# A decoder trunk in split fp32: the gated block's high part one flush later, weight sums a tile earlier, and a new order for the operand of layer 1

## The chip, the core and the metric

The kernel is one program on one core of a Trainium2 chip. A core has TensorE (PE in the profile, its weight loads PEld), VectorE (DVE), ScalarE (ACT), GpSimd (POOL) and SyncE (SP, which issues nearly all DMAs here). Each engine works through its own instructions in the order in which the program issues them; engines wait for each other through semaphores. The metric is the device time of one execution in microseconds (us), as a median over runs.

## What is computed

One inference step of a two-layer decoder for two request groups that share the weights: 1024 prompt positions and 8 x 8 sample positions, so T = 1088 columns of D = 1024 channels.

```python
for layer in range(DEPTH):                       # DEPTH = 2
    hn = rms_norm(h, norm_mix_g[layer])
    if layer % 2 == 0:                           # convolution module + stick-breaking attention
        mix, ... = conformer_sb_mixer(hn, ...)
    else:                                        # gated short convolution + causal pooling
        mix, ... = shortconv_pool_mixer(hn, ...)
    h = h + mix
    h = h + swiglu(rms_norm(h, norm_ffn_g[layer]), w_ffn_in[layer], w_ffn_out[layer])
y = rms_norm(h, norm_final_g)

def swiglu(h, w_in, w_out):
    g, u = jnp.split(h @ w_in, 2, axis=-1)
    return (jax.nn.silu(g) * u) @ w_out          # FFN_DIM = 2816
```

All inputs and outputs are fp32. Besides `y` the step returns the new keys, values and convolution and pooling states.

## The kernel before

**Split operands.** A product of fp32 operands is made as three matmuls: each operand is a high part (ScalarE's copy into the matmul format) and a low part (the operand minus its high part, by GpSimd for weights and by VectorE for activations), and `mm3` adds high by high, high by low and low by high. Activations lie with channels on the 128 partitions and positions in the free dimension. The columns are worked on as two groups, `GA` (512 columns, one block of 512) and `GB` (576 columns, two blocks of 288), in the mixer of layer 1 as one group `GT` of 1088.

**Weights.** `loads` lists every weight tile of 512 KB in the order of use, `seq` every operand made from them. `w_load` has SP fetch a tile into one of four `stage` buffers as soon as the tile that had the buffer has been read. `w_split(upto)` makes the operands `hl` (three buffers): L177 on ScalarE and L179 on GpSimd for a plain tile. `w_next` hands out the next operand and calls `w_split` so far that the operand two places on is split; so an operand is split while TensorE works two tiles before it.

**The gated channel mixer** (`run_ffn`). There are 22 tiles of 128 hidden channels, f = 0 to 21, taken in pairs. In a plain tile one product makes the gate and one the up part; VectorE scales each out of PSUM (L270, `scaled`), ScalarE takes the sigmoid-weighted gate, and `gated` puts a closure into the list `post`: multiply gate and up part on GpSimd (L430), high part on ScalarE (L431), and, put into the list `late`, low part on VectorE (L432). `flush` runs what stood in both lists when it was called; what is put into `late` meanwhile runs at the next flush. After each pair of tiles come two output tiles with four blocks each of the pair before (`out_block`, then `added`, L274 on VectorE, which adds the block to the residual `hb`), with a flush after the second block.

**Fast units.** From f = 5 on (`PLAIN`) a tile in layer 0 for `GB` and in layer 1 for both groups is made by seven products of half size instead of eight (`strassen`), 51 units in all. Its weights come as four forms r = 0 to 3 from one gate tile `sg` and one up tile `su`: sums and differences that VectorE makes (L186, L187, L188 for form 0, L191 for form 2) and then splits like other weights (L194 on ScalarE, L195 on GpSimd). The seven products (L452) fill four accumulators in this order: X (two products, form 0), Y (two, form 1), Z (two, form 2), W (one, form 3). ScalarE copies one half of Y (L468), and VectorE adds the products up in seven adds (L456): four need X and Y, two need Z, the last needs W. In program order the first four stand after Z's weights have been called for, the other three after W's. A flush stands between X and Y. There are three accumulators in PSUM, so a product waits until one is read out.

**Layer 1's operand** (`to_mixer`). With the last eight output blocks of layer 0 for `GB`, each finished channel tile n of `hb` is parked in memory, squared, and made into `x1[n]`: `prep` issues ScalarE's high part (L351) and queues VectorE's low part (L354) in `lowq`, once for the columns of `GB` and once for those of `GA`; `low(n)` works the queue down to n entries.

Of the kernel before, what the change touches and what calls it, by code (L numbers as in the profile page):

```python
# [8 lines left out]
F = mybir.dt.float32  # L9
# [9 lines left out]
NS = 64  # L19
# [10 lines left out]
def f32(ap):  # L30
    return ap.bitcast(F)
# [27 lines left out]
def trunk_kernel(ctx, tc, x_prompt, x_sample, cache_k, cache_v, state_conformer, state_shortconv, state_pool,  # L59
# [36 lines left out]
    def pc(c):  # L96
        return par[:, c:c + 1]
# [70 lines left out]
    def w_split(upto):  # L168
        while nxt[1] < min(upto, len(seq)):
            i = nxt[1]  # L170
            w_load(need(i + 1))
            a, b, r = seq[i]
            hl = wpool.tile([128, 2, 1024], FR, name="hl", bufs=3)
            lo, hi = slice(0, 512), slice(512, 1024)
            if b is None:
                st = stage.pop(a)
                act.activation(hl[:, 0], st, AF.Copy)  # L177
                for c in (lo, hi):
                    pool.tensor_tensor(hl[:, 1, c], st[:, c], f32(hl[:, 0, c]), op=OP.subtract)  # L179
                hls[i] = hl.rearrange("p s (k n) -> p s k n", k=loads[a][1])  # L180
            else:
                sg, su = stage[a], stage[b]
                if r == 0:
                    sums["a"], sums["b"] = (sums["p"].tile([128, n], F, name=f"sum{n}") for n in (1024, 512))
                    sa, sb = sums["a"], sums["b"]
                    dve.tensor_tensor(sb[:, lo], su[:, lo], su[:, hi], op=OP.add)  # L186
                    dve.tensor_tensor(sa[:, hi], sg[:, lo], su[:, lo], op=OP.subtract)  # L187
                    dve.tensor_tensor(sa[:, lo], sb[:, lo], sg[:, lo], op=OP.subtract)  # L188
                sa, sb = sums["a"], sums["b"]
                if r == 2:  # L190
                    dve.tensor_tensor(sa[:, hi], sg[:, hi], sa[:, lo], op=OP.subtract)  # L191
                src = ((sa[:, lo], sa[:, hi]), (sb[:, lo], sg[:, lo]), (su[:, hi], sg[:, hi]), (sa[:, hi],))[r]
                for c, x in zip((lo, hi), src):
                    act.activation(hl[:, 0, c], x, AF.Copy)  # L194
                    pool.tensor_tensor(hl[:, 1, c], x, f32(hl[:, 0, c]), op=OP.subtract)  # L195
                if r == 3:
                    stage.pop(a), stage.pop(b)
                hls[i] = hl.rearrange("p s (f k n) -> p s f k n", f=2, k=4)
            nxt[1] += 1

    wj = [0]

# [75 lines left out]
    late = []  # L278

    def flush():  # L280
        todo, low_parts = post[:], late[:]
        post.clear()
        late.clear()
        for f in todo + low_parts:
            f()

    K0 = list(range(KC))
# [58 lines left out]
        while len(lowq) > n:  # L346
            lowq.pop(0)()

    def prep(g, x, n, gain, squares=False, c0=0):
        o, i = x[n][:, :, c0:c0 + g.n], hb[:, n, g.cs]  # L350
        act.activation(o[:, 0], i, AF.Copy, scale=gain)  # L351
        if squares:
            add_squares(g, i, n == 0)
        lowq.append(lambda: dve.scalar_tensor_tensor(o[:, 1], i, gain, f32(o[:, 0]), op0=OP.mult, op1=OP.subtract))  # L354
# [47 lines left out]
    def run_ffn(g, accs, ps, hidp, x, last, sig=False, slot=lambda: None, forms=None):  # L402
        G = NF // 2
        n = g.n
        hid = {}
        gate = {}

        def ev_g(a):
            t = tmp()
            scaled(g, t[:, :n], a)  # L410
            if sig:
                s = tmp()
                act.activation(s[:, :n], t[:, :n], AF.Sigmoid)
                pool.tensor_tensor(t[:, :n], t[:, :n], s[:, :n], op=OP.mult)
            else:
                act.activation(t[:, :n], t[:, :n], AF.Silu)  # L416
            gate["t"] = t

        def ev_u(f, a):
            t = tmp()  # L420
            scaled(g, t[:, :n], a)
            gated(f, t, gate.pop("t"))

        def gated(f, t, u):
            if f // 2 not in hid:
                hid[f // 2] = hidp.tile([128, 2, 2, n], FR, name="hid")
            dst = hid[f // 2][:, f % 2]

            def fin():
                pool.tensor_tensor(t[:, :n], t[:, :n], u[:, :n], op=OP.mult)  # L430
                act.activation(dst[:, 0], t[:, :n], AF.Copy)  # L431
                late.append(lambda: dve.tensor_tensor(dst[:, 1], t[:, :n], f32(dst[:, 0]), op=OP.subtract))  # L432
            post.append(fin)

        def one(f, which):
            h = w_next()
            a = accs()
            block(g, a, h, x, slot=slot)
            flush()
            ev_g(a) if which == 0 else ev_u(f, a)  # L440
            slot()

        def strassen(f):
            w2 = n // 2

            def prod(acc, h, i, b):
                for k in range(4):
                    xk = forms[b](k)  # L450
                    for s, (wi, xi) in enumerate(((0, 0), (0, 1), (1, 0))):
                        pe.matmul(acc[:, :w2], h[:, wi, i, k], xk[:, xi], start=k == 0 and s == 0,  # L452
                                  stop=k == 3 and s == 2)

            def add(out, acc, x):
                dve.tensor_tensor(out, acc[:, :w2], x, op=OP.add)  # L456

            a, b = slice(0, w2), slice(w2, n)
            X, h = accs(), w_next()
            prod(X[:, 0], h, 0, "t2")  # L460
            prod(X[:, 1], h, 1, "t3")
            flush()
            slot()
            Y, h = accs(), w_next()
            prod(Y[:, 0], h, 0, "t1")
            prod(Y[:, 1], h, 1, "b11")
            G_, U, P = tmp(), tmp(), tmp()
            act.activation(G_[:, a], Y[:, 1, :w2], AF.Copy)  # L468
            Z, h = accs(), w_next()
            prod(Z[:, 0], h, 0, "t4")  # L470
            add(U[:, a], X[:, 0], G_[:, a])
            add(U[:, b], X[:, 1], U[:, a])
            add(P[:, b], Y[:, 0], U[:, b])
            add(G_[:, b], Y[:, 0], U[:, a])
            prod(Z[:, 1], h, 1, "b21")
            W, h = accs(), w_next()
            prod(W[:, 0], h, 0, "b22")
            add(P[:, a], Z[:, 0], U[:, b])
            add(G_[:, a], Z[:, 1], G_[:, a])
            add(G_[:, b], W[:, 0], G_[:, b])  # L480
            act.activation(G_[:, :n], G_[:, :n], AF.Silu)
            gated(f, P, G_)
            slot()

        for q in range(G + 1):
            if q < G:
                for f in (2 * q, 2 * q + 1):
                    if forms and f >= PLAIN:
                        if f == PLAIN:
                            forms["switch"]()  # L490
                        strassen(f)
                        continue
                    if f == 0:
                        run_in(g, accs, x, [ev_g, lambda a: ev_u(0, a)], norm_hooks(g, ps))
                        slot()
                        continue
                    one(f, 0)
                    one(f, 1)
            if q == G:
                flush()  # L500
                flush()
                last(hid.pop(q - 1))
            elif q:
                hh = hid.pop(q - 1)
                for o in range(2):
                    h = w_next()
                    for i in range(4):
                        a = accs()
                        out_block(g, a, h, i, hh)
                        added(g, hb[:, o * 4 + i, g.cs], a)  # L510
                        if o == 0 and i == 1:
                            flush()
                        slot()
# [745 lines left out]
    acc_pool(GA, 3)  # L1259
    hstack = ExitStack()  # L1260
    hidp = hstack.enter_context(tc.tile_pool(name="hid0", bufs=2, side="right"))
    knew = consts.tile([128, 4, NS], F, name="knew")
    act.activation(knew, kall[:, :, SEQ:T], AF.Copy)

    def flow_c():
# [49 lines left out]
    def to_mixer(hh):  # L1315
# [9 lines left out]
        for o in range(2):  # L1325
            h = w_next()
            for i in range(4):
                n = o * 4 + i
                a = accs()
                out_block(GB, a, h, i, hh)  # L1330
                added(GB, hb[:, n, GB.cs], a)
                sp.dma_start(park[:, n, GB.cs], hb[:, n, GB.cs])
                add_squares(GB, hb[:, n, GB.cs], n == 0)
                prep(GB, x1, n, pc(MIXG + 8 + n), c0=HALF)
                low(1)
                prep(GA, x1, n, pc(MIXG + 8 + n))
                behind.append(lowq.pop())
        low()
        for f in behind:
            f()  # L1340
# [386 lines left out]
```

## Time and profile before

| | us |
|---|---|
| median of 3 runs (lowest, highest) | 2681.61 (2680.7, 2682.34) |
| the profiled execution, its own time | 2677.37 |
| span of the profiled execution, first to last instruction | 2675.2 |
| TensorE busy in it | 2540.1 |
| VectorE, GpSimd, ScalarE busy | 1637.9, 1569.5, 1084.8 |
| mean granted TensorE clock | 0.988 |

A row of the timeline has the start, the length, the engine, the line of the kernel, what is written from what with its shape, and how many instructions are merged (x12); in brackets stand the idle time of the engine ahead of it and what ended that. A row of the list of waits has who waited for whom, the total in us, how often, and the longest wait. A row of groups has the count, the busy time, the mean in ns, and the idle time with its releasers. The row "GB/s" has the DMA rate in 40 equal slices of the window asked for.

### The profile page before, as it was taken

To read this page: it belongs to the slowest core of one execution; us is meant where nothing else is said; L and a number is where in the kernel's file an instruction comes from. 1 tells how busy PE (TensorE), PEld (TensorE's weight loads), DVE (VectorE), ACT (ScalarE), POOL (GpSimd) and SP (SyncE) were. 2 spreads that over 40 slices of the span, in tenths; PEclk is the share of its full clock that TensorE was granted. 3 is DMA by queue.
4 is the path that set the end of the run, shared out by engine and by line. 5 is a ranking of instruction groups with operands and counts; after the bars stand their busy time and mean duration, and the time that the engine had idled before them with its cause. 6 is when DMAs were issued, how large, how long until landed. Compare 5 with 4: busy or idle time off the path is not lost. (4 is left out here: it accounts for less than half of the span.)

```text
span 2675.2 us, 40716 instructions
## 1 busy us (share of the span) xinstructions
PE 2540.1 (95%) x15627; PEld 2257.4 (84%) x15627; DVE 1637.9 (61%) x2262; ACT 1084.8 (41%) x1814; POOL 1569.5 (59%) x1199
## 2 busy tenths in 40 slices
PE   8989998999999998999999899999999999999998
PEld 6788877887666656999999899998788888999997
DVE  3774776868756634377666633333666676666665
ACT  5436766744343324343333422122333334333333
POOL 6756244444333337478788722234788887677875
PEclk9999999999999999999999999999999999999999
DMA  7332241234445434322332411131232333233232
GB/s 218 114 97 71 62 112 36 71 112 117 142 142 152 119 110 128 89 72 80 95 95 87 128 44 40 42 113 34 87 93 87 90 95 95 67 104 107 85 90 75
DMA packets 346008, 254.06 MB, mean 95 GB/s; under 512 B 22657, under 2 KB 295169, under 8 KB 345800
## 3 DMA queue, kind: packets, MB, share of 16 engines
q1 hardware_dynamic: 345784, 251.46, 32.1%
q8 instruction: 124, 2.03, 0.3%
q14 instruction: 68, 0.56, 0.1%
q10 hardware_dynamic: 32, 0.01, 0.0%
HBM read 233.21 MB, written 18.69 MB: 94 GB/s over the span
## 5 line engine op out<-in xcount | busy, mean ns | idle before, releaser
L179 POOL TENSOR_TENSOR hl<-stage,hl 128x512 fp32r<-128x512 f32 x484 | 667.6, 1405 | 481.5 <-ACT hl L177 323.7
L214 PE MATMUL acc<-x,hl 128*128 128x288 f32 (+1 forms) x3792 | 710.1, 340 | 12.0 <-DVE hb L274 7.4
L214 PEld LDWEIGHTS acc<-x,hl 128*128 128x128 f32 x3792 | 585.0, 190 | 98.7 <-issue 35.3
L214 PE MATMUL acc<-hid,hl 128*128 128x288 f32 (+1 forms) x3072 | 551.0, 335 | 35.3 <-DVE hb L274 23.6
L214 PEld LDWEIGHTS acc<-hid,hl 128*128 128x128 f32 x3072 | 465.1, 190 | 105.8 <-DVE hb L274 35.1
L274 DVE TENSOR_TENSOR hb<-acc,hb 128x512 f32<-128x512 f32 (+2 forms) x376 | 263.6, 717 | 224.2 <-PE acc L214 222.1
L195 POOL TENSOR_TENSOR hl<-sum,hl 128x512 fp32r<-128x512 f32 x204 | 282.8, 1403 | 172.6 <-ACT hl L194 167.1
L452 PE MATMUL acc<-tt,hl 128*128 128x288 f32 (+1 forms) x2448 | 331.6, 291 | 0.6 <-ACT hl L194 0.3
L452 PEld LDWEIGHTS acc<-tt,hl 128*128 128x128 f32 x2448 | 321.0, 189 | 1.9 <-ACT hl L194 0.6
L177 ACT ACTIVATE hl<-stage 128x1024 fp32r<-128x1024 f32 x242 | 252.0, 1052 | 142.7 <-PE acc L214 100.9
L214 PE MATMUL acc<-x1t,hl 128*128 128x364 f32 (+1 forms) x1728 | 293.8, 331 | 7.4 <-DVE x1t L354 4.1
L214 PEld LDWEIGHTS acc<-x1t,hl 128*128 128x128 f32 x1728 | 288.9, 190 | 9.3 <-DVE x1t L354 4.4
L452 PE MATMUL acc<-x,hl 128*128 128x288 f32 (+1 forms) x1836 | 256.9, 292 | 18.0 <-ACT hl L177 12.9
L456 DVE TENSOR_TENSOR tmp<-acc,tmp 128x288 f32<-128x288 f32 (+1 forms) x357 | 146.5, 442 | 202.7 <-ACT tmp L468 157.9
L452 PEld LDWEIGHTS acc<-x,hl 128*128 128x128 f32 x1836 | 243.8, 190 | 20.8 <-ACT hl L177 19.2
L195 POOL TENSOR_TENSOR hl<-stage,hl 128x512 fp32r<-128x512 f32 x153 | 229.7, 1524 | 20.8 <-ACT hl L194 10.5
L270 DVE TENSOR_TENSOR tmp<-acc,rr 128x512 f32<-128x512 f32 (+3 forms) x128 | 89.7, 712 | 204.7 <-PE acc L214 189.2
L194 ACT ACTIVATE hl<-sum 128x512 fp32r<-128x512 f32 x204 | 122.1, 623 | 186.1 <-DVE sum L188 119.1
L431 ACT ACTIVATE hid<-tmp 128x512 fp32r<-128x512 f32 (+1 forms) x88 | 57.9, 657 | 326.6 <-POOL tmp L430 326.5
L231 POOL TENSOR_TENSOR ss<-ss,tmp 128x512 f32<-128x512 f32 (+2 forms) x62 | 105.2, 1696 | 87.8 <-ACT tmp L230 84.4
L430 POOL TENSOR_TENSOR tmp<-tmp 128x512 f32<-128x512 f32 (+1 forms) x88 | 125.7, 1429 | 26.4 <-ACT tmp L416 25.4
L214 PE MATMUL acc<-x1a,hl 128*128 128x512 f32 x480 | 121.3, 406 | 2.5 <-POOL hl L179 1.3
(252 smaller groups left out, 2936.4 us busy)
## 6 DMA issues: line engine op xcount, KB each, us to landing
stage<-in_w_ffn_in_dram SPq DMA_DIRECT2D x176, 512.0 KB
stage<-in_w_ffn_out_dram SPq DMA_DIRECT2D x88, 512.0 KB
stage<-in_w_in_even_dram SPq DMA_DIRECT2D x40, 512.0 KB
kst<-in_cache_k_dram SPq DMA_DIRECT2D x64, 256.0 KB
vst<-in_cache_v_dram SPq DMA_DIRECT2D x64, 256.0 KB
stage<-in_w_out_even_dram SPq DMA_DIRECT2D x16, 512.0 KB
stage<-in_w_in_odd_dram SPq DMA_DIRECT2D x16, 512.0 KB
park<-hb SPq DMA_DIRECT2D x16, 288.0 KB
```

Source lines behind the costliest of these rows:

```text
L177: act.activation(hl[:, 0], st, AF.Copy)
L179: pool.tensor_tensor(hl[:, 1, c], st[:, c], f32(hl[:, 0, c]), op=OP.subtract)
L194: act.activation(hl[:, 0, c], x, AF.Copy)
L195: pool.tensor_tensor(hl[:, 1, c], x, f32(hl[:, 0, c]), op=OP.subtract)
L214: pe.matmul(acc[:, b, :c1 - c0], w, x[:, xi, c0:c1], start=first and s == 0, stop=last and s == 2)
L231: pool.tensor_tensor(ss[:, g.cs], ss[:, g.cs], t[:, :g.n], op=OP.add)
L270: dve.tensor_tensor(d, a, r, op=OP.mult)
L274: dve.tensor_tensor(d, a, d, op=OP.add)
L430: pool.tensor_tensor(t[:, :n], t[:, :n], u[:, :n], op=OP.mult)
L431: act.activation(dst[:, 0], t[:, :n], AF.Copy)
L452: pe.matmul(acc[:, :w2], h[:, wi, i, k], xk[:, xi], start=k == 0 and s == 0, stop=k == 3 and s == 2)
L456: dve.tensor_tensor(out, acc[:, :w2], x, op=OP.add)
```

## The change

Three edits and a small one.

*Flush.* `fin` now issues only the multiply and puts both parts of the split into `late`, so that the high part (ScalarE) moves from right behind the multiply to the next flush, where it stands with the low part (VectorE). `flush` itself does what it did.

*Weight sums.* After an operand has been split, `w_split` looks at the next one. If that is a form 0, its tiles are called for and two of its three sums are issued there. The third sum stays at form 0. Form 2's sum gets a tile of its own (`sum_c`) where it used to overwrite half of `sum1024`.

*Layer 1's operand.* One high part over all 1088 columns takes the place of two; the low parts are queued for `GB` and `GA` of each channel tile, and from the third tile on `GA`'s is put off until all blocks are done. `prep` loses its argument `c0`.

*Memory.* `knew` moves from the constants into a pool that ends with layer 0's work on `GA`.

```diff
@@ w_split
             else:
                 sg, su = stage[a], stage[b]
+                sa, sb = sums["a"], sums["b"]
                 if r == 0:
-                    sums["a"], sums["b"] = (sums["p"].tile([128, n], F, name=f"sum{n}") for n in (1024, 512))
-                    sa, sb = sums["a"], sums["b"]
-                    dve.tensor_tensor(sb[:, lo], su[:, lo], su[:, hi], op=OP.add)
-                    dve.tensor_tensor(sa[:, hi], sg[:, lo], su[:, lo], op=OP.subtract)
                     dve.tensor_tensor(sa[:, lo], sb[:, lo], sg[:, lo], op=OP.subtract)
-                sa, sb = sums["a"], sums["b"]
                 if r == 2:
-                    dve.tensor_tensor(sa[:, hi], sg[:, hi], sa[:, lo], op=OP.subtract)
-                src = ((sa[:, lo], sa[:, hi]), (sb[:, lo], sg[:, lo]), (su[:, hi], sg[:, hi]), (sa[:, hi],))[r]
+                    sums["c"] = sums["p"].tile([128, 512], F, name="sum_c")
+                    dve.tensor_tensor(sums["c"], sg[:, hi], sa[:, lo], op=OP.subtract)
+                src = ((sa[:, lo], sa[:, hi]), (sb[:, lo], sg[:, lo]), (su[:, hi], sg[:, hi]), (sums.get("c"),))[r]
...
             nxt[1] += 1
+
+            a, b, r = seq[min(i + 1, len(seq) - 1)]
+            if b is not None and r == 0:
+                w_load(b + 1)
+                sg, su = stage[a], stage[b]
+                sums["b"] = sums["p"].tile([128, 512], F, name="sum512")
+                dve.tensor_tensor(sums["b"], su[:, lo], su[:, hi], op=OP.add)
+                sums["a"] = sums["p"].tile([128, 1024], F, name="sum1024")
+                dve.tensor_tensor(sums["a"][:, hi], sg[:, lo], su[:, lo], op=OP.subtract)
@@ gated
             def fin():
                 pool.tensor_tensor(t[:, :n], t[:, :n], u[:, :n], op=OP.mult)
-                act.activation(dst[:, 0], t[:, :n], AF.Copy)
-                late.append(lambda: dve.tensor_tensor(dst[:, 1], t[:, :n], f32(dst[:, 0]), op=OP.subtract))
+                late.append(lambda: split(dst, t[:, :n]))
             post.append(fin)
@@ to_mixer
                 add_squares(GB, hb[:, n, GB.cs], n == 0)
-                prep(GB, x1, n, pc(MIXG + 8 + n), c0=HALF)
+                gain = pc(MIXG + 8 + n)
+                act.activation(x1[n][:, 0], hb[:, n], AF.Copy, scale=gain)
+                for gr in (GB, GA):
+                    lowq.append(lambda gr=gr, n=n, gain=gain: dve.scalar_tensor_tensor(
+                        x1[n][:, 1, gr.cs], hb[:, n, gr.cs], gain, f32(x1[n][:, 0, gr.cs]), op0=OP.mult,
+                        op1=OP.subtract))
+                if n > 1:
+                    behind.append(lowq.pop())
                 low(1)
-                prep(GA, x1, n, pc(MIXG + 8 + n))
-                behind.append(lowq.pop())
         low()
         for f in behind:
             f()
```

More of the change, by code (lines that the diff above doesn't have):

```diff
@@ L280, in flush @@
     def flush():
-        todo, low_parts = post[:], late[:]
+        todo = post + late
         post.clear()
         late.clear()
-        for f in todo + low_parts:
+        for f in todo:
             f()
@@ L347, in low, with prep @@
             lowq.pop(0)()
-    def prep(g, x, n, gain, squares=False, c0=0):
-        o, i = x[n][:, :, c0:c0 + g.n], hb[:, n, g.cs]
+    def prep(g, x, n, gain, squares=False):
+        o, i = x[n][:, :, :g.n], hb[:, n, g.cs]
         act.activation(o[:, 0], i, AF.Copy, scale=gain)
@@ L1261, in trunk_kernel @@
     hidp = hstack.enter_context(tc.tile_pool(name="hid0", bufs=2, side="right"))
-    knew = consts.tile([128, 4, NS], F, name="knew")
+    knew = hstack.enter_context(tc.tile_pool(name="knewp", bufs=1, side="right")).tile([128, 4, NS], F, name="knew")
     act.activation(knew, kall[:, :, SEQ:T], AF.Copy)
```

## The prediction

> **What bounds the kernel now.** I read the page first, then the list of who waited for whom on TensorE, then the order of time in one period of each stage that the change touches.
>
> ```profile
> span 2675.2 us, 40716 instructions
> PE 2540.1 (95%) x15627; PEld 2257.4 (84%) x15627; DVE 1637.9 (61%) x2262; ACT 1084.8 (41%) x1814; POOL 1569.5 (59%) x1199
> ```
> ```profile
> PE acc L214 <- DVE hb L274: 34.0, 33, 5.2
> PE acc L452 <- ACT hl L177: 12.9, 9, 2.1
> PE acc L214 <- DVE x1t L354: 4.1, 1, 4.1
> ```
>
> PE is busy 95% of the span, so time can only come from its waits. The three above (total, count, longest) are what the change aims at: the output blocks that wait for `added` (L274), the last product of a fast unit in group A of layer 1, and the first low part of layer 1's operand.
>
> Below is one period of that group A stage. I call the four accumulators of a fast unit X, Y, Z, W, and the eight output blocks that follow every second unit o1 to o8. Three accumulators exist; by the order of release W takes X's, o1 Y's, o2 Z's, o3 W's, o4 that of o1.
>
> ```profile
> 2029.44 3.82 POOL L195 TENSOR_TENSOR hl<-sum,hl 128x512 fp32r<-128x512 f32 x3 [2.13 <-ACT hl L194]
> 2033.21 4.26 POOL L195 TENSOR_TENSOR hl<-stage,hl 128x512 fp32r<-128x512 f32 x3
> 2037.43 1.30 POOL L430 TENSOR_TENSOR tmp<-tmp 128x512 f32<-128x512 f32 x1
> 2039.99 1.27 POOL L195 TENSOR_TENSOR hl<-sum,hl 128x512 fp32r<-128x512 f32 x1 [1.26 <-ACT hl L194]
> 2041.26 5.93 POOL L179 TENSOR_TENSOR hl<-stage,hl 128x512 fp32r<-128x512 f32 x4
> ```
> ```profile
> 2036.85 1.60 PE L452 MATMUL acc<-tt,hl 128*128 128x256 f32 x12
> ...
> 2038.29 1.60 PE L452 MATMUL acc<-x,hl 128*128 128x256 f32 x12
> 2038.76 0.63 ACT L431 ACTIVATE hid<-tmp 128x512 fp32r<-128x512 f32 x1 [5.34 <-POOL tmp L430]
> 2039.30 0.61 ACT L194 ACTIVATE hl<-sum 128x512 fp32r<-128x512 f32 x1
> ...
> 2040.21 2.43 DVE L456 TENSOR_TENSOR tmp<-acc,tmp 128x256 f32<-128x256 f32 x6 [6.40 <-ACT tmp L468]
> 2041.24 1.66 PE L452 MATMUL acc<-x,hl 128*128 128x256 f32 x12 [1.36 <-ACT hl L177]
> ...
> 2042.74 4.42 PE L214 MATMUL acc<-hid,hl 128*128 128x512 f32 x18
> ...
> 2043.28 1.06 DVE L186 TENSOR_TENSOR sum<-stage 128x512 f32<-128x512 f32 x1
> ...
> 2044.27 1.77 DVE L187 TENSOR_TENSOR sum<-stage 128x512 f32<-128x512 f32 x1
> 2045.96 1.78 DVE L188 TENSOR_TENSOR sum<-sum,stage 128x512 f32<-128x512 f32 x1
> 2047.66 1.27 DVE L274 TENSOR_TENSOR hb<-acc,hb 128x512 f32<-128x512 f32 x2
> 2048.39 7.27 PE L214 MATMUL acc<-hid,hl 128*128 128x512 f32 x30 [1.24 <-DVE hb L274]
> ```
>
> The reader is to see two stalls. PE stands 1.36 us before W: ScalarE waits 5.34 us at L431 for GpSimd's multiply L430, its split L194 comes behind, and GpSimd's low part of that form ends only at 2041.26, when W starts (so I read the name L177 in the row as the wrong one). Then o1, o2, o3 run (18 matmuls, 1.33 us a block) and o4 stands 1.24 us, because VectorE makes three sums for the next unit (L186 to L188) before the first `added`.
>
> **The change part by part.** *Flush.* The high part moves from behind the multiply to the flush after it. In this period L431 leaves ScalarE's queue at that place; L194 can run as soon as X is done, and GpSimd's last low part follows L430 at once: 2037.43 + 1.30 + 1.27 = 2040.00 instead of 2041.26. Z's last product ends at 2038.29 + 1.60 = 2039.89. So W starts at 2040.0 and ends at 2041.4, and ScalarE's evacuation of Y (L468) no longer waits behind L431: Y is complete at 2036.9, and four adds of 0.41 us are done by about 2039.0.
>
> *Sums a tile ahead.* L186 and L187 are now issued when the second output tile is split, which is at the call for W's weights. On VectorE's in-order queue that is behind the first four adds and **ahead of the two adds that free Z**, while L188 stays ahead of `added`. What these sums need is the pair of weight tiles just being loaded:
>
> ```profile
> 2037.50 0.37 SPq L159 DMA_DIRECT2D stage<-in_w_ffn_in_dram  x1
> ```
> ```profile
> GB/s 0 0 0 0 0 76 139 160 254 293 334 348 338 258 209 182 209 287 311 301 240 135 53 43 25 0 0 0 0 0 0 0 0 33 0 41 76 190 266 317
> ```
>
> SP issues the second tile at 2037.50, when GpSimd has read the last of the old one (2033.21 + 4.26 = 2037.47). The second row is the DMA rate in quarter microseconds from 2036: bytes flow until 2042.25. The tile is thus there between 2042.25 and 2043.28, where L186 reads it today without a wait; I take 2042.65. Nothing in the change moves that issue: `w_load` for this pair was called earlier in both versions, and GpSimd's six splits from 2029.44 to 2037.47 stand back to back.
>
> So VectorE, idle from 2039.0, waits until 2042.65, and Z's two adds behind it. The sums have three prices: 1.06 and 1.77 above, both beside GpSimd, and 0.68 in this row of the last stage:
>
> ```profile
> 2396.88 0.68 DVE L186 TENSOR_TENSOR sum<-stage 128x512 f32<-128x512 f32 x1
> ```
>
> GpSimd's four L179 start 1.26 us earlier and still last until about 2045.9, so I take 1.5 + 1.77. Z is free at 2042.65 + 1.5 + 1.77 + 2 x 0.41 = 2046.75. PE has finished o1 at 2041.4 + 1.33 = 2042.75 and **stands about 4 us before o2**; o4 then begins at 2046.8 + 2 x 1.33 = 2049.5. Today it is 2048.39. Both old stalls go, one larger comes: **+1.1 us**. With sums at 1.06 + 1.2 and landing at 2042.25 it is -0.3, with 1.78 twice and landing at 2043.0, +1.7. Behind o4 nothing is late: L188 and `added` take 1.4 us after W's last add, and o4 wants them at 2049.4.
>
> [...]
>
> The same in layer 0, group B, and layer 1, group B:
>
> ```profile
> 1396.12 4.95 PE L214 MATMUL acc<-hid,hl 128*128 128x288 f32 x36
> 1401.48 0.80 PE L214 MATMUL acc<-hid,hl 128*128 128x288 f32 x4 [0.41 <-DVE hb L274]
> ```
> ```profile
> GB/s 0 0 0 20 113 174 242 322 303 301 332 240 201 207 215 223 317 320 285 158 125 119 12 0 0 0 0 0 0 0 0 0 0 0 8 94 158 190 299 317
> ```
> ```profile
> 2451.28 4.92 PE L214 MATMUL acc<-hid,hl 128*128 128x288 f32 x36
> ...
> 2451.86 1.83 DVE L186 TENSOR_TENSOR sum<-stage 128x512 f32<-128x512 f32 x1
> ...
> 2456.71 8.20 PE L214 MATMUL acc<-hid,hl 128*128 128x288 f32 x60 [0.51 <-DVE hb L274]
> ```
> ```profile
> GB/s 0 0 0 0 0 0 0 0 23 82 158 285 330 283 309 348 283 213 225 229 252 315 317 287 139 107 76 0 0 0 0 0 0 0 0 0 0 0 0 16
> ```
>
> There is no stall before W here, and a block takes 1.59 us. Bytes flow until 1394.75 (the row starts at 1389) and 2449.75 (it starts at 2443); with 0.4 us more the sums start at 1395.15 and 2450.15. Z is free 1.5 + 1.77 + 0.9 later, at 1399.3 and 2454.3; two blocks on, o4 begins at 1402.5 and 2457.5 instead of 1401.48 and 2456.71: **+1.0 and +0.8 us**.
>
> Each stage has eight such places: 8 x (1.1 + 1.0 + 0.8) = +23.2. Two of the eight in the last stage lie beside transposes of finished rows and have no stall today:
>
> ```profile
> 2378.76 3.33 PE L214 MATMUL acc<-hid,hl 128*128 128x288 f32 x24
> ```
> ```profile
> GB/s 0 0 139 352 221 328 131 145 223 205 188 236 227 258 277 264 311 346 336 324 324 225 129 33 18 2 0 0 0 0 0 0 0 0 0 0 66 0 0 0
> ```
>
> There bytes flow until 2378.5, Z is free at about 2382.6, and o2 starts today at 2378.76 + 1.59 = 2380.35: 2.2 us instead of 0.8, twice +1.4. The last unit of group A has its stall before W and no sums behind it: -1.3.
>
> Before the *other* unit of a pair the sums keep their order on VectorE, since nothing of that engine stands between the old place and the new. The separate tile for the fourth form takes away a wait; the new flush adds one, L432 behind L431 in the same flush:
>
> ```profile
> L187 DVE TENSOR_TENSOR sum<-stage 128x512 f32<-128x512 f32 x51 | 63.4, 1243 | 29.7 <-POOL hl L195 29.7
> L431 ACT ACTIVATE hid<-tmp 128x512 fp32r<-128x512 f32 (+1 forms) x88 | 57.9, 657 | 326.6 <-POOL tmp L430 326.5
> ```
>
> 29.7 us over 51 sums, mostly 1.2 us in every second, against up to 0.66 us for the copy: behind L432 stand the sums and `added`. I set both at zero together, from -0.5 to +0.6 a pair. In the plain stages ScalarE gets the 3.7 us a flush back that it waits at L431, with PE hardly waiting for it: -2, from -8 to +6.
>
> *Layer 1's operand.*
>
> ```profile
> 1532.37 0.74 PE L214 MATMUL acc<-x1t,hl 128*128 128x364 f32 x3 [2.88 <-DVE hb L274]
> 1537.17 3.09 PE L214 MATMUL acc<-x1t,hl 128*128 128x364 f32 x9 [4.07 <-DVE x1t L354]
> ```
> ```profile
> 1531.22 0.67 ACT L230 ACTIVATE tmp<-hb 128x576 f32<-128x576 f32 x1
> ```
> ```profile
> L219 ACT ACTIVATE x1t<-hb x8: 1098/1102/1115, 1741.4 to 1749.2; 128x1088 fp32r<-128x1088 f32 x8
> ```
>
> PE runs three matmuls and stands 4.07 us for the first low part of group A's columns. The change makes that part early, so this wait goes. But ScalarE's one copy of 1088 columns (1.10 us by the like L219) precedes it, and in the first two columns VectorE must wait for square and copy of the same column (0.7 + 1.1) before its next `added`. Two such waits, 3.6 us, move the end of the eighth `added` from 1532.3 to 1535.9; PE starts at 1536.0 and runs on, where today's start at 1537.17 has three matmuls (0.5 us) behind it: -0.7, from -4.3 (all gained) to +2. `knew` only changes its pool: nothing.
>
> **Sum:** 23.2 + 2.8 - 1.3 - 2 - 0.7 = +22.0. The profiled execution took 2677.37 us (2.2 beside its span), 4.2 under the median of 2681.61; added to the median: **2703.6 us**.
>
> **The rivals.** *The sums find their tile* (faster). If both tiles were there when VectorE comes to them, the old stalls would simply go: in group A 8 x 2.6 + 1.4, in the group B stages some 14 x 0.45, with the last two terms -31: 2651. It decides at a landing before 2042.75 - 0.82 - 3.27 = 2038.7, four microseconds ahead of the rows; smaller gains come from sums at 0.68 each (o4 at 2047.5 in group A). For it: GpSimd's splits would have to move, and L187's lost wait frees up to 1.2 us of them. Against it: the rate rows. *Balance:* partly hidden sums (1.06 + 1.2) and an early landing, about 0 a place, which leaves the small terms: 2678. *VectorE late in every unit:* L432 waits 0.6 us in each of 24 pairs and L188, the next form and X come as much later: +14, 2718; against it, the wait lost at L187.
>
> **How the numbers follow.** About 0.2%, 5.4 us, is what a measurement can tell from no change. Forecast 0.56 (2690 to 2715), VectorE late 0.14, balance 0.16, faster 0.14. Slower is 0.70. The range, 2680 to 2722, leaves out the faster case and the ends: landing and sums at their bounds are worth -1.4 to +0.6 a place, -34 to +14 over 24, of which the lower half is given to the rivals.
>
> **What would show it.** Right: L186's successor starts with a wait for a DMA, ends ahead of the two Z adds (L456's successor), and PE stands 1 to 4 us before o2 with that add as releaser, 24 times; no stall before W in group A; no 4 us wait for x1t. Wrong: PE waits for `acc` shrink below 34 us, or VectorE reaches the sums after their tile.

## The result and the profile after

| | before | after |
|---|---|---|
| median of 4 runs (lowest, highest), us | 2681.15 (2680.61, 2682.34) | 2699.32 (2696.44, 2705.41) |
| ratio to before, 95% interval | | 1.007 [1.0051, 1.0089] |
| profiled execution, its own time, us | 2677.37 | 2697.51 |
| span, us | 2675.2 | 2695.6 |
| mean granted TensorE clock | 0.988 | 0.982 |

The change makes the kernel slower by 0.7%: 18.2 us by the medians, 20.4 by the spans. The forecast was +22.0 us (2703.6, range 2680 to 2722). The kernel after moves the lines: products are L457 (before L452), their seven adds L461 (L456), output blocks L220 (L214), `added` L280 (L274), `scaled` L276 (L270); the two sums made ahead are L203 and L205 (L186, L187), the third is L185 (L188).

The page after (the span, then the busy time of each engine):

```profile
span 2695.6 us, 40688 instructions
PE 2550.9 (95%) x15627; PEld 2269.7 (84%) x15627; DVE 1624.9 (60%) x2262; ACT 1089.1 (40%) x1806; POOL 1573.5 (58%) x1199
```

and TensorE's list of waits (who waited for whom, total, times, longest):

```profile
PE acc L220 <- DVE tmp L461: 42.3, 24, 3.6
PE acc L220 <- DVE hb L280: 19.3, 10, 5.2
```

All three waits that the change aimed at shrink or go: 34.0 to 19.3 us for `added`; the row of 12.9 us before W is gone (0.61 us is left, in group A's first fast unit), and so are the 4.1 us for layer 1's operand. In their place stands one that did not exist: 24 output blocks wait 42.3 us for VectorE's adds, at the 24 places where sums are made behind output tiles. PE is also *busy* 10.8 us longer with the same 15627 matmuls. A longer busy time at the same count needs a cause of its own; it comes below.

One period of group A in layer 1, first TensorE and then VectorE (start, length, what, and in brackets the idle time ahead and its releaser):

```profile
2040.71 3.04 PE L457 MATMUL acc<-x,hl 128*128 128x256 f32 x24
2043.59 1.57 PE L220 MATMUL acc<-hid,hl 128*128 128x512 f32 x6
2047.43 8.90 PE L220 MATMUL acc<-hid,hl 128*128 128x512 f32 x37 [2.28 <-DVE tmp L461]
```
```profile
2039.89 1.77 DVE L461 TENSOR_TENSOR tmp<-acc,tmp 128x256 f32<-128x256 f32 x4 [4.08 <-ACT tmp L473]
2044.34 0.70 DVE L203 TENSOR_TENSOR sum<-stage 128x512 f32<-128x512 f32 x1 [2.68 <-DMA stage<-in_w_ffn_in_dram]
2044.97 1.75 DVE L205 TENSOR_TENSOR sum<-stage 128x512 f32<-128x512 f32 x1
2046.64 1.07 DVE L461 TENSOR_TENSOR tmp<-acc,tmp 128x256 f32<-128x256 f32 x3
```

Z and W run as one group of 24 matmuls without a stall between them. VectorE has done four adds by 2041.66, stands 2.68 us for the weight tile, makes the two sums, and only then Z's adds. PE has finished o1 and stands 2.28 us before o2, released by such an add. This is the order that the prediction wrote down; its numbers differ, as shown below.

The same in layer 1's group B:

```profile
2470.51 1.75 PE L220 MATMUL acc<-hid,hl 128*128 128x288 f32 x12
2472.95 9.25 PE L220 MATMUL acc<-hid,hl 128*128 128x288 f32 x68 [0.69 <-DVE tmp L461]
```
```profile
2469.42 1.05 DVE L203 TENSOR_TENSOR sum<-stage 128x512 f32<-128x512 f32 x1 [1.14 <-DMA stage<-in_w_ffn_in_dram]
2470.39 1.77 DVE L205 TENSOR_TENSOR sum<-stage 128x512 f32<-128x512 f32 x1
```

and at a place beside transposes of finished rows:

```profile
2389.68 1.75 PE L220 MATMUL acc<-hid,hl 128*128 128x288 f32 x12
2393.76 2.98 PE L220 MATMUL acc<-hid,hl 128*128 128x288 f32 x12 [2.33 <-DVE tmp L461]
2396.53 1.06 PE L1617 MATMUL m<-ident,hb 128*128 128x128 f32 x4
2397.24 5.14 PE L220 MATMUL acc<-hid,hl 128*128 128x288 f32 x36
2402.22 0.60 PE L1617 MATMUL m<-ident,hb 128*128 128x128 f32 x4
```

Compare rows of one shape: twelve matmuls take 1.75 us before the stall and 2.98 us after it, and four transposes take 1.06 and, 6 us later, 0.60 us. The table of windows of this kernel (window, its length, busy time and count of PE, PEld, DVE, ACT, POOL, then the granted clock, DMA share and GB/s) shows why:

```profile
2388.00:2394.10 6.10, 3.77 (x28) 3.54 (x28) 4.44 (x6) 1.06 (x1) 4.05 (x3) 1.00 0.09 24
2394.10:2397.50 3.40, 3.40 (x17) 3.39 (x16) 1.96 (x4) 2.40 (x4) 2.01 (x2) 0.50 0.03 5
2397.50:2402.00 4.50, 4.50 (x36) 4.50 (x36) 3.26 (x5) 1.09 (x2) 2.79 (x3) 1.00 0.30 92
```

For 3.4 us behind the stall the granted clock is 0.50. PE is busy in all of it, but its matmuls of 288 columns start every 0.24 us there and every 0.13 us ahead of the stall and from 2397.6 us on, so such a stretch costs 1.5 us by that pitch, and up to 1.7 us by the clock alone. Adding up these stretches over the whole span, before has 62.9 us at half clock and after 96.7 us. But for the one that the end of the span cuts off, they come in lengths of 3.4 and 6.8 us. In the part of the trace with layer 1's fast units, after has nine such lengths that before has not: six in group A (one of them double) and three in group B, 30.6 us, worth up to 15.3 us. There they stand behind all four stalls of 3.25 to 3.6 us and behind four of the seven of 2.26 to 2.38 us, and behind none of the short ones (0.67 to 0.8 us). Layer 0 has one more of 2.34 us and seven of 0.67 to 1.96 us at these places, and none of them has half clock behind it.

Layer 1's operand, after:

```profile
1526.82 5.42 PE L220 MATMUL acc<-hid,hl 128*128 128x288 f32 x36 [1.35 <-DVE hb L280]
1537.27 8.93 PE L220 MATMUL acc<-x1t,hl 128*128 128x364 f32 x43 [5.03 <-DVE hb L280]
```

One stall of 5.03 us, with a new one of 1.35 us ahead of it, takes the place of 2.88 and 4.07 us: the 4 us wait went, and its time came back.

### The profile page after: what moved, and what is told of

It reads as the page before. It is cut to its first block, busy times and chain, and to the rows that moved or that the text cites. A ratio compares the mean times of both kernels' runs of the same rounds, so it can differ in the third digit from the quotient of the medians.

```text
span 2695.6 us, 40688 instructions
## 1 busy us (share of the span) xinstructions
PE 2550.9 (95%) x15627; PEld 2269.7 (84%) x15627; DVE 1624.9 (60%) x2262; ACT 1089.1 (40%) x1806; POOL 1573.5 (58%) x1199
## 5 line engine op out<-in xcount | busy, mean ns | idle before, releaser
L179 POOL TENSOR_TENSOR hl<-stage,hl 128x512 fp32r<-128x512 f32 x484 | 672.1, 1413 | 479.7 <-ACT hl L177 336.3
L220 PE MATMUL acc<-x,hl 128*128 128x288 f32 (+1 forms) x3792 | 708.3, 340 | 11.8 <-DVE hb L280 7.9
L220 PEld LDWEIGHTS acc<-x,hl 128*128 128x128 f32 x3792 | 584.0, 190 | 97.7 <-issue 38.4
L220 PE MATMUL acc<-hid,hl 128*128 128x288 f32 (+1 forms) x3072 | 567.4, 341 | 64.9 <-DVE tmp L461 42.3
L220 PEld LDWEIGHTS acc<-hid,hl 128*128 128x128 f32 x3072 | 479.4, 195 | 136.7 <-DVE tmp L461 49.3
L280 DVE TENSOR_TENSOR hb<-acc,hb 128x512 f32<-128x512 f32 (+2 forms) x376 | 268.4, 720 | 268.9 <-PE acc L220 267.4
L457 PE MATMUL acc<-tt,hl 128*128 128x288 f32 (+1 forms) x2448 | 331.6, 291 | 0.3 <-POOL hl L192 0.3
L457 PEld LDWEIGHTS acc<-tt,hl 128*128 128x128 f32 x2448 | 321.0, 189 | 1.3 <-POOL hl L192 0.5
L220 PE MATMUL acc<-x1t,hl 128*128 128x364 f32 (+1 forms) x1728 | 293.6, 331 | 5.5 <-DVE hb L280 5.0
L220 PEld LDWEIGHTS acc<-x1t,hl 128*128 128x128 f32 x1728 | 289.0, 190 | 7.0 <-ACT x1t L1340 5.2
L192 POOL TENSOR_TENSOR hl<-sum,hl 128x512 fp32r<-128x512 f32 x153 | 205.2, 1362 | 113.7 <-ACT hl L191 113.7
L457 PE MATMUL acc<-x,hl 128*128 128x288 f32 (+1 forms) x1836 | 253.0, 291 | 4.0 <-DVE tmp L461 3.3
L461 DVE TENSOR_TENSOR tmp<-acc,tmp 128x288 f32<-128x288 f32 (+1 forms) x357 | 146.8, 440 | 165.2 <-ACT tmp L473 122.1
L457 PEld LDWEIGHTS acc<-x,hl 128*128 128x128 f32 x1836 | 242.0, 189 | 4.6 <-ACT hl L177 3.8
L276 DVE TENSOR_TENSOR tmp<-acc,rr 128x512 f32<-128x512 f32 (+3 forms) x128 | 89.7, 712 | 185.3 <-PE acc L220 175.7
L191 ACT ACTIVATE hl<-sum 128x512 fp32r<-128x512 f32 x153 | 91.0, 626 | 124.2 <-PE acc L220 62.4
L191 ACT ACTIVATE hl<-stage 128x512 fp32r<-128x512 f32 x153 | 89.8, 618 | 118.3 <-PE acc L220 113.8
L226 DVE TENSOR_TENSOR hid<-tmp,hid 128x512 fp32r<-128x512 f32 (+1 forms) x88 | 97.4, 1107 | 61.6 <-ACT hid L225 60.3
```

Of the source, the lines that this page charges most:

```text
L220: pe.matmul(acc[:, b, :c1 - c0], w, x[:, xi, c0:c1], start=first and s == 0, stop=last and s == 2)
L226: dve.tensor_tensor(dst[:, 1], src, f32(dst[:, 0]), op=OP.subtract)
L276: dve.tensor_tensor(d, a, r, op=OP.mult)
L280: dve.tensor_tensor(d, a, d, op=OP.add)
```

## The experiments

Ten kernels ran, in three comparisons, each with the kernel before on the same chip.

| label | what it is | median, us (lowest, highest) | ratio to before, 95% interval |
|---|---|---|---|
| sums_only | before + the weight sums | 2697.43 (2691.07, 2699.19) | 1.0057 [1.0043, 1.0071] |
| flush_only | before + the flush | 2651.78 (2650.41, 2652.84) | 0.9889 [0.9874, 0.9904] |
| operand_only | before + the operand | 2678.78 (2674.97, 2681.72) | 0.9991 [0.9982, 1.0] |
| no_tile_wait | after, sums without their tile | 2644.43 (2641.11, 2648.39) | 0.9863 [0.9848, 0.9878] |
| flush_operand | after without the sums | 2653.23 (2650.54, 2655.88) | 0.9896 [0.9882, 0.991] |
| inner_only | after, sums ahead only inside a pair | 2653.01 (2648.45, 2657.31) | 0.9898 [0.9883, 0.9914] |
| between | flush, operand, sums among the blocks | 2658.83 (2650.11, 2660.72) | 0.9915 [0.9899, 0.993] |
| keep_clock | after + unread matmuls in group A | 2693.02 (2685.86, 2698.76) | 1.0046 [1.0031, 1.006] |
| keep_all | the same, and three places of group B | 2689.58 (2684.34, 2695.59) | 1.0037 [1.0024, 1.0049] |
| after_again | after, beside keep_all | 2705.36 (2696.11, 2706.54) | 1.0091 [1.0076, 1.0107] |

The kernel before had 2680.9 us in the comparison of the first four, 2680.71 in that of the next four, 2681.3 in that of the last two.

### One part at a time

**sums_only** is before with the edit of `w_split` and the move of `knew`.

> The kernel before with the sums a tile ahead (and form 2's own tile), nothing else. Theory: the whole loss comes from here. VectorE reaches L186's successor before the next weight tile has landed, two adds that free accumulator Z stand behind it, TensorE stands before the second output block, and where it stands over 2 us a half-clock window of 3.4 us follows: +10 to +25 us over the kernel before. Group A of layer 1 is the worst, since its stall before W stays as well. Rival (the flush makes the loss, by ScalarE's and VectorE's later split): within 4 us of the kernel before.

It ran at +16.5 us. Its list of waits (L220, L280 and L462 are output blocks, `added` and the seven adds; L458 is the products):

```profile
PE acc L220 <- DVE tmp L462: 29.3, 24, 3.3
PE acc L220 <- DVE hb L280: 18.1, 11, 5.2
PE acc L458 <- ACT hl L177: 9.3, 9, 2.1
```

So this one edit brings the 24 waits, and alone it makes nearly the whole loss. The stall before W, which this edit leaves, remains at 9.3 us. "Over 2 us" in the expectation says more than the trace of after: of its twelve stalls of 2.26 to 3.60 us at these places, eight have a stretch at half clock behind them.

**flush_only** is before with this:

```diff
-                act.activation(dst[:, 0], t[:, :n], AF.Copy)
-                late.append(lambda: dve.tensor_tensor(dst[:, 1], t[:, :n], f32(dst[:, 0]), op=OP.subtract))
+                late.append(lambda: split(dst, t[:, :n]))
```

> The kernel before with the high part of the gated block at the next flush, nothing else. Theory: the eight or nine stalls of 1.36 us before W in group A of layer 1 go, but the sums there start with the landing of their tile, so that most of it comes back before the fourth output block: -2 to -8 us against before, and TensorE's waits for L456 and L274 tell where. Rival (the flush makes the loss): +8 us or more, with TensorE waiting for units whose form 0 is late.

It ran at −29.1 us, far below what I expected. The same group A period, TensorE and then GpSimd (products L451 here):

```profile
2028.30 3.04 PE L451 MATMUL acc<-x,hl 128*128 128x256 f32 x24
2031.18 4.41 PE L214 MATMUL acc<-hid,hl 128*128 128x512 f32 x18
2036.98 7.26 PE L214 MATMUL acc<-hid,hl 128*128 128x512 f32 x30 [1.39 <-DVE hb L274]
```
```profile
2027.17 1.30 POOL L430 TENSOR_TENSOR tmp<-tmp 128x512 f32<-128x512 f32 x1
2028.42 1.30 POOL L195 TENSOR_TENSOR hl<-sum,hl 128x512 fp32r<-128x512 f32 x1
2029.67 5.51 POOL L179 TENSOR_TENSOR hl<-stage,hl 128x512 fp32r<-128x512 f32 x4
```

GpSimd goes from L430 to L195 without the 1.26 us that stand between them in the rows of before, Z and W are one group, and the stall before o4 is 1.39 us where it was 1.24. The stall before W, 1.36 us in most periods, is simply gained, in every period but the first (1.81 of 2.06 us are left there): from the first to the last fast unit of group A this kernel moves 11.3 us ahead of before, by the starts of the units' first products. In group B before has stalls before W only in the first two pairs of layer 0 (2.09, 0.67 and 0.48 us; here 1.72 and none) and in the first unit of layer 1 (1.62 us, here 1.61). Yet it gains in all of group B, 6.8 us in layer 0 (up to 1.7 of it a stretch at half clock that before alone has, at 1212.8 us) and 4.6 in layer 1. These three gains make 22.7 of the 24.3 us between the two profiled spans. VectorE in layer 1's group B:

```profile
2431.48 1.04 DVE L186 TENSOR_TENSOR sum<-stage 128x512 f32<-128x512 f32 x1
2432.44 1.77 DVE L187 TENSOR_TENSOR sum<-stage 128x512 f32<-128x512 f32 x1
2434.14 0.68 DVE L188 TENSOR_TENSOR sum<-sum,stage 128x512 f32<-128x512 f32 x1
```

L186 takes 1.04 us where it took 1.83 us at its counterpart of before (2451.86): GpSimd's low part ends 1.4 us earlier against the matmuls, and the sum meets GpSimd's next instructions at another point (L179 runs from 2430.69 to 2433.67 here, from 2449.35 to 2454.84 there); that this sets its time was not shown apart. The 0.8 us that this saves is more than the 0.51 us that o4 waited there. Half clock is 69.6 us here, 62.9 before, so the gain as a whole is no effect of the clock.

**operand_only** is before with the third edit.

> The kernel before with the one high part and late low parts of layer 1's operand, nothing else. Theory: the wait of 4.07 us for the first low part goes, and about as much comes back before it, because the last block's add is later: -2 to +1 us against before. Rival (a saving of the whole wait): -4 us.

11 runs differ from the kernel before by 2.1 us of 2681, which can't be told from no change, and at the place itself the tenth matmul of the operand moves by 0.05 us.

The parts alone sum to 16.5 − 29.1 − 2.1 = −14.7 us; together they give +18.2. The flush gains 29 us alone and nothing once the sums are made ahead (2699.3 for the whole change against 2697.4 for sums_only).

### Is it the landing of the tile?

**no_tile_wait** is after with

```diff
-                dve.tensor_tensor(sums["b"], su[:, lo], su[:, hi], op=OP.add)
+                dve.tensor_tensor(sums["b"], rr[:, lo], rr[:, hi], op=OP.add)
-                dve.tensor_tensor(sums["a"][:, hi], sg[:, lo], su[:, lo], op=OP.subtract)
+                dve.tensor_tensor(sums["a"][:, hi], rr[:, lo], rr[:, hi], op=OP.subtract)
```

where `rr` is a tile that is there all the time.

> The changed kernel, but the two sums that are made a tile ahead read columns of rr, which have been there for long, in place of the next unit's weight tiles (the same shapes on the same engine; the output is no longer the reference's). Theory: the sums no longer wait for a landing, TensorE's 42 us of waiting for L461 nearly goes, and most of the half-clock windows of layer 1 with it: 2650 to 2662 us. If only the time of the sums on VectorE's queue counts and not the landing: 2680 to 2695. Rival (the flush makes the loss): 2690 or more.

It runs 55 us below after, even below its range. Its longest list entries are

```profile
PE acc L220 <- DVE hb L280: 18.2, 8, 5.2
PE acc L220 <- DVE tmp L276: 13.8, 3, 5.6
PE acc L220 <- POOL hl L179: 7.3, 12, 1.3
```

and the row for L461 is not among them. The instructions and their order are those of after; only the tile that the two sums read differs, and with it the wait for its arrival. So it is the landing that costs, not the sums' own 2.5 us of VectorE.

**flush_operand** has `w_split` as it was; **inner_only** makes the sums ahead only where the operand before is itself a form, so at the 24 places behind output tiles, and at the first fast unit of each group, which follows a plain tile, they stand as before:

```diff
-            if b is not None and r == 0:
+            if b is not None and r == 0 and seq[i][1] is not None:
```

> The changed kernel with the sums put back to where they were (flush and operand stay). The parts alone gave -29 us (flush) and -2 us (operand) against before, and +17 us (sums), while all three together gave +18. Theory: the sums undo the flush's gain wherever a weight tile is late, so that without them flush and operand simply add: 2646 to 2653 us. Rival (flush and operand disturb each other): 2660 or more.

> The changed kernel, but the two sums are made a tile ahead only for the second unit of a pair, whose form 0 follows directly on a form 3; the first unit's, behind two output tiles, are made where they were. Theory: all of the harm lies at the 24 places behind output tiles, where the tile has not landed; the inner places have theirs: within 4 us of the run with the sums put back, 2644 to 2655. Rival (the sums ahead of time harm in every unit, by standing in front of adds): 2665 or more.

The two have the same time, 2653.2 (just above its range) and 2653.0. So sums ahead inside a pair cost and gain nothing, and all the harm, 46 us on top of the other two edits, lies at the 24 places: at the three first units TensorE stands no longer before Y and W in after (1.72, 0.90 and 1.63 us) than in flush_only (1.72, 1.81 and 1.61 us).

**between** tries to have the sums early without the queue: one sum after each of the first three blocks' `added`, and form 0 split behind the third block.

> Flush and operand as in the change; the three sums for the first unit of a pair are not made ahead but one after each of the first three output blocks' adds, and form 0 is split after the third. Theory: the tile has landed, and no add of a finished block waits behind three sums in a row, so that the 1.2 to 1.6 us stalls before the fourth block in group A of layer 1 shrink below 0.5: 8 to 11 us below flush and operand alone, 2636 to 2645. Rival (VectorE is simply too busy among the output blocks, and form 0 comes too late): no better than flush and operand alone.

That fell short. In its profile the stall before o4 is gone (one period has 0.30 us before o5), but each of the eight pairs in group A has 0.77 or 0.78 us inside one of its units (L467 is the products, L471 their adds):

```profile
2016.65 1.60 PE L467 MATMUL acc<-x,hl 128*128 128x256 f32 x12
2019.02 1.67 PE L467 MATMUL acc<-x,hl 128*128 128x256 f32 x12 [0.77 <-DVE tmp L471]
```

Its runs reach from 2650 to 2661 us, and its median is no better than that of flush_operand.

### Is half clock a cost, or a label beside the stall?

**keep_clock** gives PE something to do in the stalls of group A; **keep_all** does so at the first three places of layer 1's group B as well (the edit is keep_all's; `warm` lists the pairs):

```diff
+                        if o == 0 and i == 0 and q in warm:
+                            m = ps()
+                            for _ in range(16):
+                                pe.matmul(m[:, :256], h[:, 0, 0, 0:128], hh[:, 0, 0, 0:256], start=True, stop=True)
                         if o == 0 and i == 1:
                             flush()
```

> The changed kernel, with 16 matmuls of 256 columns that nothing reads put between the first and second output block at the eight places of group A in layer 1 (1.7 to 1.9 us of TensorE work at full clock, into a stall of 2.3 us). Theory of the clock: the stall itself costs little there, the half-clock window of 3.4 us that follows most of the stalls does; with TensorE kept busy those five or six windows between 1930 and 2240 us go, and the stage ends 4 to 10 us earlier in spite of more work. Rival (the clock windows cost nothing, the wait does): the stage ends when it did or up to 3 us later.

> The changed kernel with 16 matmuls of 256 columns that nothing reads between o1 and o2, at the eight places of layer 1's group A and at the first three of its group B. Theory (a stall of over 2 us brings a stretch of 3.4 us at half clock behind it, worth up to 1.7 us): in the stages from 1910 to 2475 us the nine stretches' worth (30.6 us) of half clock go, which is up to 15.3 us; the unread matmuls lie in the stalls, and what they cost beyond is 0 to 5 us. So 8 to 14 us below the changed kernel in the same comparison, about 2685 to 2692. Rival (the half clock is only a label beside a wait that would last as long anyway): the same time as the changed kernel or up to 10 us above it, since eleven times 1.7 us of matmuls are added.

> The changed kernel as it is, beside the one before it in this list and on the same chip, so that the two can be compared. Every theory: 2694 to 2706 us, ratio to the kernel before 1.005 to 1.009, with about ten more half clock stretches than the kernel before.

The windows from 1913 to 2473 us, first of after, then of keep_all:

```profile
1913.00:2473.00 560.00, 517.94 (x3484) 485.08 (x3482) 359.32 (x492) 209.37 (x338) 415.10 (x293) 0.97 0.30 88
```
```profile
1913.00:2473.00 560.00, 536.15 (x3759) 507.42 (x3759) 368.28 (x504) 214.39 (x347) 422.54 (x299) 1.00 0.30 89
```

The granted clock is 1.00 instead of 0.97, and over the whole span half clock falls from 96.7 us (in after and in after_again) to 64.0 us. keep_all runs 15.8 us below after_again on the same chip (12 by the two profiled executions), with intervals that lie apart, although it does 176 matmuls more; expected were 8 to 14. Of those 12 us, 7.0 lie in the two stages that have the unread matmuls and 4.0 in layer 0's fast units, where the two kernels do the same, so a part of the difference is one between executions; against the profile of after the two stages gain 13.6 us. So half clock is a cost, about half or more of what the change loses against before: with it held off, 0.37% [0.24, 0.49] remains of 0.91% [0.76, 1.07]. Of the 46 us that the sums cost beside the other two edits it is about a third. keep_clock alone had brought group A's fast units 2.9 us ahead of after from the first to the last (4.7 us up to the first of group B), though its total doesn't stand apart from that of after by their intervals.

What would show the rest of the mechanism, a tile that lands earlier with the sums where the change has them, was not tried, so that step is inferred from no_tile_wait and inner_only.

## Why the prediction was right in sign and size, and where its steps were wrong

The shifts of the starts of the fast units' first products, after against before in the two profiled executions, give a ledger by stage. It is set against the prediction's terms:

| | predicted, us | measured, us |
|---|---|---|
| plain stages up to the first fast unit (flush, ScalarE freed) | −2, with the fourth row | −0.9 |
| layer 0, group B: eight places | 8 x 1.0 = +8.0 | +1.7 |
| layer 1's operand | −0.7 | +0.1 |
| from there to layer 1's first fast unit, plain stages | in the first row | −1.2 |
| layer 1, group A: eight places, the last unit | 8 x 1.1 − 1.3 = +7.5 | +7.7 |
| layer 1, group B: eight places, two beside transposes | 8 x 0.8 + 2.8 = +9.2 | +12.8 |
| end | 0 | +0.2 |
| sum | +22.0 | +20.4 |

**Right: the order and the wait.** The two sums stand ahead of Z's adds, the first waits for the tile, PE stands before o2 with that add as releaser, 24 times; from its second unit on nothing stalls before W in group A; the 4 us wait for the operand's low part is gone. no_tile_wait shows the landing as the cause, inner_only the place. The plain stages give about the −2 us that was booked for them. Of the rivals, "the sums find their tile" is what no_tile_wait makes by force, and it gives 2644 where 2651 was worked out. "Balance" and "VectorE late in every unit" didn't come: the rival of a late VectorE was priced on L432 behind L431, and flush_only, which has that order in every unit, is 29 us faster.

**Mis-sized: a clean place.** The prediction took landing 2042.65 + 1.5 + 1.77 + 0.82 = 2046.75 for Z in group A. After is 2.42 us later at that unit, so that is 2049.17 on its scale, and o2 starts at 2047.43. The tile is there 0.7 us sooner than assumed (2044.34 against 2045.07, with SP issuing the second load 0.4 us sooner against the unit), and the first sum takes 0.70 us, not 1.5: while it runs one GpSimd instruction ends (at 2044.50), and the next then takes 1.71 us where its two forerunners took 1.30 and 1.29. The second sum takes 1.75 as assumed. (The seven adds of this unit take 0.405 to 0.425 us each, with GpSimd at work beside them; 0.41 was assumed.) So o4 begins 16.6 us after the unit's start, where it was 17.3: a clean place is worth −0.6 us instead of +1.1. In layer 1's group B the sums start where predicted (2469.42 against 2450.15 + 19.23 = 2469.38, the unit being 19.23 us later in after) and the first takes 1.05 us: +0.2 instead of +0.8. In group A that is below even the lower end that the prediction gave (−0.3); of the prices 0.68, 1.06 and 1.77 it had taken one near the middle, and the lower two were right for the first sum. In layer 0 the first two pairs gain 1.6 us: before has stalls before W there (2.09, 0.67 and 0.48 us), where the prediction saw none, and the stretch at half clock at 1212.8 us. The other six places cost 3.3 us, 0.55 each instead of 1.0.

**Missing: the clock.** The prediction says that time can only come from TensorE's waits, and its sum counted waits in a clock that stays. In after it doesn't: up to 15.3 of the 20.5 us that layer 1's two fast stages lose are half clock. keep_all, which has none there, ends these stages 6.9 us later than before by the two profiles, its unread matmuls included, where the prediction had +16.7. In group A the places without it would be near −0.8 to −2.5 us in all (an estimate: 7.7 less 8.5 by the pitch of the matmuls in the six stretches, or less 10.2 at 1.7 each), while the ledger says +7.7, by chance the +7.5 that was predicted. The two errors, places too dear by some 14 to 18 us (an estimate: each ledger row less its half clock, against the prediction) and no term for the clock of about 13 to 15, nearly cancelled. That the forecast came within 4 us of the measured time is therefore luck; its sign is not (keep_all, without that half clock, is still 0.37% slower than before), nor is the order that it named.

**Mis-sized: the places beside transposes.** The prediction had 2.2 us each. The wait is 2.33 us, so that step held, and the clock adds 1.5 to 1.7: the units move by 4.15 us at each of the two, and by 3.5 at the pair ahead of them, which the prediction had counted as clean.

**Mis-priced: the flush.** It was booked at −2 outside the places and, inside them, only as a stall that makes room for a larger one. No sum was made for the flush alone. It is worth −29 us by the medians, and the prediction's own row showed the largest piece: 1.36 us before W, eight times and once more. What hides it in after is that o2 may not begin before landing, sums and Z's adds, however early W ends: one block of cover stands between W and o2, where three stand between W and o4.

**Small: the operand.** −0.7 predicted within −4.3 to +2, and nothing that can be measured came; the later high parts, each over 1088 columns (1.19 us; VectorE stands 5.0 us for them, 2.3 for those of before), give back what the wait was.

## What to carry to other kernels

Before work is moved ahead in an engine's queue, look at when its input lands and at what stands behind it there: here VectorE stood 2.68 us for a tile with Z's adds behind it in its queue, since two sums that would wait harmlessly behind three blocks of matmuls were put ahead of the adds that free an accumulator, with one block to cover the wait. Try the parts of a change one by one, since their effects don't add: one edit alone gave −29 us, another +16.5, and together with a third that did nothing they gave +18; the kernel to keep is flush_only, 1.1% faster than before. And price a stall of TensorE as long as these at its length plus a stretch at half clock behind it, 1.5 to 1.7 us here: at the 24 places of after it followed half of the stalls of 2.26 to 2.38 us and all of those of 3.25 to 3.6 us.

## What the runs showed of the hardware that was not expected

- At the 24 places of after, TensorE's granted clock fell to 0.50 for 3.4 us behind stalls of 2.26 to 2.38 us in four of eight cases, behind every one of 3.25 to 3.6 us (once for 6.8 us), and behind none of 0.67 to 1.96 us. Why the middle ones differ among themselves these runs don't settle. 16 unread matmuls of 256 columns in each of 11 of these waits kept the clock at 1.00 in layer 1's fast stages (1913 to 2473 us; 0.97 in after).
- An elementwise sum of two 128 x 512 tiles on VectorE takes 0.70 us at one place (L203 at 2044.34, as one GpSimd instruction ends and the next begins) and 1.75 us right behind it (L205, beside a GpSimd instruction of 1.71 us). Which of the two prices holds for the first sum decides the sign of a place: with 1.75 us the −0.6 us of the group A place would be an estimated +0.5.
